# A hybrid conv layer on one Trainium2 core: thirteen rows of norm factors reach all partitions by a store and a repeating load, where a TensorE matmul had spread them

## The chip, the cores and the metric

The kernel runs on one core of one Trainium2 chip. Five engines matter, and each works through its own instruction list in order: TensorE (PE in the profile, with weight loads shown apart as PEld), VectorE (DVE), ScalarE (ACT), GpSimd (POOL) and SyncE (SP), whose instructions here are nearly all DMA issues. The metric is the device time of one execution in microseconds (us). The kernel before takes 1971.13 us, the median of 3 runs that lie between 1970.71 and 1971.24.

## The reference

One layer with a short gated convolution as its token mixer, then a dense SwiGLU feed-forward block, on a sequence of 2048 tokens with 1024 channels in float32. Each of the two sublayers has an RMS norm ahead of it and another behind it, and a shift, a scale and a gate that come from a conditioning vector:

```python
h = modulate(rms_norm(x, norm_gains[i, 0]), sh_m, sc_m)
h = short_conv_mixer(h, conv_w_in[j], conv_w[j], conv_w_out[j])
x = x + g_m[:, None, :] * rms_norm(h, norm_gains[i, 1])
h = modulate(rms_norm(x, norm_gains[i, 2]), sh_f, sc_f)
h = swiglu(h, ffn_w_gate_up[i], ffn_w_down[i])
x = x + g_f[:, None, :] * rms_norm(h, norm_gains[i, 3])
```

An RMS norm needs one number for each token, 1/sqrt(mean of the squares of its 1024 channels). What this case is about is how that number gets from where it is computed to where it is multiplied in.

## The kernel before

**Tiles and stages.** Activations are held channel-major: 128 channels on the partitions, 512 tokens in the free dimension. The 2048 tokens are two units `u` of two groups of 512 (`tok`). The stages run in the order `in0`, `out0`, `in1`, `out1` (the mixer's two projections for unit 0, then unit 1), `gu0`, `down0`, `gu1`, `down1` (the feed-forward block). Each product is a fast block scheme with seven products instead of eight (P1 to P7), and each float32 operand is split in a high and a low part, so that one block product of 128x128 by 128x512 takes three matmuls of reduced precision (`fp32r`).

**Order.** The order on every engine is written out by the program. It runs over a list of slots; one slot is one product, at most 12 matmuls. `later` and `yield n` put a step n slots further on, and the steps that fall due are written out ahead of or behind a slot's matmuls. Weights are fetched some slots ahead of their use (`WHOLE, BLOCKS, SUMS, HIGH, LOW = 5, 9, 7, 5, 4`: whole pairs of high and low part 5 slots ahead, raw blocks 9, the cast to the high part by ACT 5, the low part by DVE 4). Loads and most stores are issued by SP, in that one order, some stores by ACT. The issuing engine waits ahead of an issue for the data, for the buffer and for an earlier DMA: the DMAs of SP and ACT share eight completion counters in turn, and an issue waits until the DMA that had its counter before has landed.

**Norm factors.** The sums of squares of 512 tokens come out with the tokens on the partitions, as a tile of 128x4. `root` turns them into the factors `q`, 128x4 (POOL's power, then three short DVE instructions). The multiplication, though, needs all 512 factors in every partition, as a tile `rb` of 128x512, in a pool with two buffers (`NRB`). `spread_later` does that: DVE writes four diagonal matrices of 128x128 side by side (`diagonal`, names ending in `d`), `lag` slots later TensorE multiplies a matrix of ones with them into a PSUM bank (`spread`, names ending in `b`), and ACT copies the bank to `rb` (names ending in `r`). It is used thirteen times:

- `r2`, `r3` (from `norm_of_rows`): norm ahead of the mixer, unit 1, while `in0` and `out0` run; `lag` is 6.
- `n00`, `n01`, `n10`, `n11` (from `after_out`): norm behind the mixer, in the stages `in1` and `gu0`; `lag` is 4.
- `h00`, `h01`, `h10`, `h11`: norm ahead of the feed-forward block, at the ends of `out1` and `down0`, from factors named `m`; `lag` is 4.
- `o00`, `o01`, `o10` (from `after_down`): norm behind the feed-forward block; `lag` is 4, for `o10` it is 2.

Three more rows of factors are spread elsewhere by TensorE (`r0`, `r1` at the start, `last` at the end). All instructions carry line 78, that of a helper, so names have to tell them apart.

Of the kernel before, what the change touches and what calls it, by code (L numbers as in the profile page):

```python
# [10 lines left out]
F32 = mybir.dt.float32  # L11
# [4 lines left out]
P = 128  # L16
# [7 lines left out]
CH = 512  # L24
# [11 lines left out]
NBIG, NWP, NRAW, NTMP, NRB = 17, 7, 16, 10, 2  # L36
# [13 lines left out]
def hybrid_conv_layer(  # L50
# [31 lines left out]
    V, A, PE, G, SP = map(Engine, (nc.vector, nc.scalar, nc.tensor, nc.gpsimd, nc.sync))  # L82
# [4 lines left out]
    bigs, pairs, raws, sb = (ctx.enter_context(tc.tile_pool(name=n, bufs=1)) for n in ("bigs", "pairs", "raws", "sb"))  # L87
# [12 lines left out]
    def tmp(name):  # L100
        return sb.tile([P, CH + 2], F32, tag="tmp", bufs=NTMP, name=name)
# [4 lines left out]
    def bank(name):  # L106
        return ps.tile([P, CH], F32, tag="mm", bufs=8, name=name)
# [128 lines left out]
    def diagonal(q, name):  # L236
        dg = tmp(name + "d")
        for t in range(4):
            V.tensor_scalar(dg[:, t * P : (t + 1) * P], ident, q[:, t : t + 1], None, ALU.mult)
        return dg  # L240

    def spread(dg, name):
        ps_ = bank(name + "b")
        PE.matmul(ps_, one, dg[:, :CH], start=True, stop=True)
        rb = sb.tile([P, CH], F32, tag="rb", bufs=NRB, name=name + "r")
        A.copy(rb, ps_)
        return rb

    def spread_later(q, name, put, lag=4):
        dg = diagonal(q, name)  # L250
        yield lag
        put(spread(dg, name))

    def norm_of_sums(acc, name):

# [8 lines left out]
    def norm_of_rows(g, name, put):  # L264
        s = [small(4, f"{name}a{i}") for i in range(2)]
        rows = [(t, i) for t in range(4) for i in range(2)]
        xr = {}

        def load(k):
            if k < len(rows):  # L270
                t, i = rows[k]
                xr[k] = raw(f"xr{g}{t}{i}")
                r0 = g * CH + t * P
                SP.dma_start(xr[k], x[r0 : r0 + P, i * CH : (i + 1) * CH])

        load(0)
        yield 2
        for k, (t, i) in enumerate(rows):
            load(k + 1)
            yield 2  # L280
            A.activation(xr[k], xr[k], AF.Square, scale=1.0 / 32.0, accum_out=s[i][:, t : t + 1])
        yield 1
        v = small(4, name + "v")
        V.tensor_tensor(v, s[0], s[1], ALU.add)
        V.tensor_scalar(v, v, EPS, None, ALU.add)
        yield 1
        q = yield from root(v, name)
        yield 1
        yield from spread_later(q, name, put, 6)


    def scratch(shape, name):
        return dram.tile(shape, F32, name=name)
# [598 lines left out]
    for s in slots:  # L892
        ph = s.ph
        if ph.kind in ("out", "down"):
            w = Weight(ph.kind, s.grp, s.op, None, ks=s.ks)
        elif s.n < LEAD and ph.name != "in0" or ph.name == "in1" and s.g.i == 2:
            w = Weight(ph.kind, s.grp, s.op, None)
        else:
            b = of.setdefault((ph.name, s.n), Blocks(ph.kind, s.grp))
            w = Weight(ph.kind, s.grp, s.op, b, ph.name == "in0" and s.g.i in (1, 2),  # L900
                       whole_words=ph.name == "in0" and s.n < LEAD and s.op in UNSPLIT)
# [3 lines left out]
        if s.n >= LEAD and extra.get(ph.name) and len(position) > 7 * LEAD + 2 * (EARLY - LEAD):  # L905
            n = count[ph.name] = count.get(ph.name, 0) + 1
# [26 lines left out]
    def put(d, key, rb):  # L933
        d[key] = rb

    def after_out(ph, tok):
# [4 lines left out]
        q = yield from norm_of_sums(ph.acc[tok], f"n{u}{tok}")  # L941
        yield (24 if u == 0 else 34) + 8 * tok
        yield from spread_later(q, f"n{u}{tok}", partial(put, rb, 0))
        acc = {}
        tiles = {}
# [23 lines left out]
    def after_down(ph, tok):  # L969
# [8 lines left out]
        if not ph.last:  # L978
            yield 22 + 10 * tok
        yield from spread_later(q, f"o{u}{tok}", partial(put, rb, 0), 2 if ph.last else 4)  # L980
        tiles = {}

# [370 lines left out]
    for ph in phases[1:]:  # L1353
# [18 lines left out]
        else:  # L1372
            rb = {}
# [105 lines left out]
```

## Time and profile before

| | before |
|---|---|
| time, median of 3 runs | 1971.13 us |
| the profiled execution, first to last instruction | 1972.0 us |
| PE busy | 1940.5 us (98%), 8460 matmuls |
| DVE busy | 1466.1 us (74%), 2159 instructions |
| ACT busy | 871.4 us (44%), 1430 instructions |
| POOL busy | 340.7 us (17%) |
| DMA | 459.51 MB, mean 233 GB/s |
| granted TensorE clock, mean | 0.997 |

The span of the profiled execution runs from its first to its last instruction; the profile gives no time around it, and it lies 0.9 us above the median of the runs. Busy shares are means over stages with different limits. The views that say more are the busy time by stretches, the chain that ended last (what each step waited for, followed back from the end) and the order of single instructions in a few places.

### The profile page before, as it was taken

The numbers are of one execution on the slowest core, as the hardware profiler recorded it, in microseconds if no ns is written. First come the engines' busy times: TensorE is split into PE (matmuls) and PEld (weight loads), VectorE is DVE, ScalarE is ACT, GpSimd is POOL, SyncE is SP. The second block draws the span as 40 slices with busy tenths as digits, with TensorE's granted clock in tenths as the row PEclk, the third lists the DMA queues.
The fourth block names the chain that finished last, engine by engine and source line by source line (L and its number), as shares of the span: only waits on it lengthen the run. The fifth ranks groups of instructions, "written<-read, shape, count | busy, mean of one in ns | idle before, by whom it ended". The sixth has DMA issues, their size and how long they took to land.

```text
span 1972.0 us, 24969 instructions
## 1 busy us (share of the span) xinstructions
PE 1940.5 (98%) x8460; PEld 1573.3 (80%) x8460; DVE 1466.1 (74%) x2159; ACT 871.4 (44%) x1430; POOL 340.7 (17%) x224
## 2 busy tenths in 40 slices
PE   7899999999999999999999999999999999999998
PEld 4578887777888888888888888888888888888886
DVE  4898888988998876898776755586776655665466
ACT  4543447534345653444333454463333333444452
POOL 0012202201221311243341310120100100111010
PEclk9999999999999999999999999999999999999999
DMA  9369859869996763677665887578564342386634
GB/s 389 126 224 374 312 187 350 320 226 367 327 320 221 272 245 126 231 238 244 210 221 190 295 291 269 188 272 277 187 197 141 122 145 97 115 313 228 199 134 132
DMA packets 204752, 459.51 MB, mean 233 GB/s; under 512 B 22864, under 2 KB 38352, under 8 KB 198224
## 3 DMA queue, kind: packets, MB, share of 16 engines
q1 hardware_dynamic: 180000, 403.52, 59.3%
q10 hardware_dynamic: 24624, 54.40, 7.2%
q8 instruction: 66, 1.08, 0.2%
q14 instruction: 62, 0.51, 0.1%
HBM read 326.75 MB, written 131.07 MB: 232 GB/s over the span
## 4 chain that ended last, share of the span: by engine, by line
PE 84%; DVE 6%; DMA 5%; issue 2%; ACT 2%; SPq 0%; POOL 0%; ACTq 0%; POOLq 0%; DVEq 0%
PE gu0P L78 21%; PE gu1P L78 21%; PE in0P L78 11%; PE down0P L78 11%; PE down1P L78 9%; PE in1P L78 5%; PE out1P L78 4%; PE out0P L78 1%; DMA kgu2P<-gu2P 1%; DVE ada L78 1%; DVE in1c L78 1%; DVE in1y L78 0%; DMA y1S<-in1b1s 0%; DMA in0a<-xt_d 0%; DMA c<-c_row_d 0%
## 5 line engine op out<-in xcount | busy, mean ns | idle before, releaser
L78 DVE TENSOR_TENSOR gu1a<-gu1P,gu1a 128x512 f32<-128x512 f32 x63 | 43.5, 691 | 108.6 <-PE gu1P L78 108.6
L78 DVE TENSOR_TENSOR gu0a<-gu0P,gu0a 128x512 f32<-128x512 f32 x63 | 43.3, 688 | 70.5 <-PE gu0P L78 68.5
L78 POOL TENSOR_TENSOR gu1a<-gu1a 128x512 f32<-128x512 f32 x11 | 19.0, 1728 | 363.4 <-DVE gu1g11s L78 42.5
L78 ACT COPY gu1a<-gu1P 128x512 f32<-128x512 f32 x42 | 24.7, 589 | 98.5 <-PE gu1P L78 87.3
L78 POOL TENSOR_TENSOR nq<-nq,nq 128x512 f32<-128x512 f32 x28 | 42.5, 1517 | 129.9 <-ACT nq L78 125.1
L78 ACT COPY gu0a<-gu0P 128x512 f32<-128x512 f32 x42 | 24.5, 588 | 83.7 <-PE gu0P L78 82.5
L78 DVE CUSTOM_DVE_ANT_0 ada<-ada,c 128x512 f32<-128x512 f32 x80 | 56.8, 720 | 0.0
L78 ACT COPY gu1g<-gu1P 128x512 f32<-128x512 f32 x24 | 14.1, 589 | 92.8 <-PE gu1P L78 92.8
L78 POOL TENSOR_TENSOR down0q<-down0q,down0q 128x512 f32<-128x512 f32 x14 | 23.9, 1705 | 144.1 <-ACT down0q L78 144.0
L78 ACT COPY gu0g<-gu0P 128x512 f32<-128x512 f32 x24 | 14.1, 589 | 76.9 <-PE gu0P L78 75.4
L78 POOL TENSOR_TENSOR gu0a<-gu0a 128x512 f32<-128x512 f32 x11 | 18.3, 1660 | 171.1 <-ACT gu0a L78 47.4
L78 POOL TENSOR_TENSOR down1q<-down1q,down1q 128x512 f32<-128x512 f32 x10 | 16.1, 1610 | 148.7 <-ACT down1q L78 148.6
L78 DVE TENSOR_TENSOR gu1g<-gu1P,gu1g 128x512 f32<-128x512 f32 x24 | 16.6, 692 | 27.4 <-ACT gu1g L78 26.0
L78 DVE TENSOR_TENSOR down2P<-down2P,down2P 128x512 fp32r<-128x512 f32 x14 | 11.9, 853 | 28.6 <-ACT down2P L78 28.6
L78 ACT ACTIVATE gu1a<-gu1a 128x512 f32<-128x512 f32 x42 | 26.6, 633 | 13.2 <-DVE xo L78 6.0
L78 ACT ACTIVATE gu0a<-gu0a 128x512 f32<-128x512 f32 x42 | 26.6, 634 | 11.1 <-DVE gu0a L78 9.3
L78 POOL TENSOR_TENSOR out1q<-out1q,out1q 128x512 f32<-128x512 f32 x14 | 22.3, 1592 | 52.0 <-ACT out1q L78 51.9
L78 POOL TENSOR_TENSOR out0q<-out0q,out0q 128x512 f32<-128x512 f32 x14 | 23.1, 1647 | 44.1 <-ACT out0q L78 44.0
L78 DVE TENSOR_TENSOR xx<-xx,zz 128x512 f32<-128x512 f32 x32 | 28.1, 878 | 1.1
L78 ACT ACTIVATE nq<-xx 128x512 f32<-128x512 f32 x32 | 20.2, 632 | 17.1 <-DVE xx L78 17.0
L78 DVE TENSOR_TENSOR gu0g<-gu0P,gu0g 128x512 f32<-128x512 f32 x24 | 16.5, 689 | 14.7 <-ACT gu0g L78 13.3
L78 DVE TENSOR_TENSOR down10P<-down10P,down10P 128x384 fp32r<-128x384 f32 x14 | 8.6, 615 | 22.3 <-ACT down10P L78 22.3
(3225 smaller groups left out, 6733.5 us busy)
## 6 DMA issues: line engine op xcount, KB each, us to landing
ada<-ada_d SPq DMA_DIRECT2D x64, 256.0 KB, 5.7
act0A<-gu0a SPq DMA_DIRECT2D x33, 256.0 KB, 3.4
act1A<-gu1a SPq DMA_DIRECT2D x33, 256.0 KB, 2.5
ada<-ada_d SPq DMA_DIRECT2D x16, 512.0 KB, 9.4
zz<-z SPq DMA_DIRECT2D x32, 256.0 KB, 5.3
xx<-xt_d SPq DMA_DIRECT2D x32, 256.0 KB, 5.4
x<-xx ACTq DMA_DIRECT2D x32, 256.0 KB, 5.5
down0S<-act0S SPq DMA_DIRECT2D x8, 1024.0 KB, 7.0
```

What stands on the lines that cost most here:

```text
L78: return tc.keep_in_program_order(f(*args, **kwargs))
```

## The change

`spread_later` no longer builds diagonals. It takes a row of 512 floats in device memory, issues from SP a store of the 128x4 factors into it (so that token t·128+p lands at that position: 512 pieces of 4 bytes), and `lag - 1` slots later a load, again from SP, that repeats the row in all 128 partitions of `rb` (128 rows of 2 KB, 256 KB). One slot after that `rb` is handed on, at the same slot as before.

```diff
     def spread_later(q, name, put, lag=4):
-        dg = diagonal(q, name)
-        yield lag
-        put(spread(dg, name))
+
+        row = scratch([CH], name + "w")
+        SP.dma_start(row.rearrange("(t p) -> p t", p=P), q)
+        yield lag - 1
+        rb = sb.tile([P, CH], F32, tag="rb", bufs=NRB, name=name + "r")
+        SP.dma_start(rb, row.rearrange("(a n) -> a n", a=1).to_broadcast((P, CH)))
+        yield 1
+        put(rb)
```

In all, 13 matmuls of 128x512 (each on the profile as two), 52 diagonal blocks on DVE and 13 copies on ACT go; 26 DMAs on SP come. Nothing else changes its order on any engine.

TensorE, near the end of the stage `down1`, around the spread of `o10` (numbers behind names are buffers). Before:

```order
L78 MATMUL down1P_2_15693<-down1S31h,down6P_15671 128x512 x2
L78 MATMUL down1P_2_15693<-down1S_15575,down6P_15671 128x512
L78 MATMUL o10b<-o10d,one 128x512
L78 MATMUL down1P_3_15719<-down1S31h,down7P_15689 128x512 x2
L78 MATMUL down1P_3_15719<-down1S_15575,down7P_15689 128x512
```

After:

```order
L78 MATMUL down1P_2_15633<-down1S31h,down6P_15611 128x512 x2
L78 MATMUL down1P_2_15633<-down1S_15515,down6P_15611 128x512
L78 MATMUL down1P_3_15659<-down1S31h,down7P_15629 128x512 x2
L78 MATMUL down1P_3_15659<-down1S_15515,down7P_15629 128x512
L78 MATMUL down1P_3_15659<-down1S31h,down7P_15629 128x512 x2
```

The spread stood between the products of two groups, and they now follow one another.

SP, at the same place. `down1A` are feature loads, `down1P` to `down9P` weight blocks, `xo` the residual for the output. Before:

```order
L78 DMA down1A_15737<-act1A_123 128x2048
L78 DMA down8P_15754<-kdown8P_9341 128x384
L78 DMA down1A_15759<-act1A_123 128x2048
L78 DMA down1P_15782<-kdown1P_7935 128x512
L78 DMA down1A_15789<-act1A_123 128x1536
L78 DMA down5P_15803<-kdown5P_8741 128x512
L78 DMA xo_15815<-x_134 128x512
L78 DMA down9P_15829<-kdown9P_9554 128x384
```

After:

```order
L78 DMA down1A_15677<-act1A_123 128x2048
L78 DMA down8P_15694<-kdown8P_9301 128x384
L78 DMA down1A_15699<-act1A_123 128x2048
L78 DMA o10w<-o10q 128x4x1
L78 DMA down1P_15719<-kdown1P_7895 128x512
L78 DMA down1A_15726<-act1A_123 128x1536
L78 DMA o10r<-o10w 128x512
L78 DMA down5P_15742<-kdown5P_8701 128x512
L78 DMA xo_15750<-x_134 128x512
L78 DMA down9P_15764<-kdown9P_9514 128x384
```

The store `o10w` waits for the factors `o10q` and stands ahead of a weight block and the third feature load; the load `o10r` waits for the store to land, two issues later, and stands ahead of all that follows.

SP again, in the stage `in1`, around `n01`. `in7P…k` are pairs of weights, `in2b` raw weight blocks, `zz` and `xx` inputs of the residual sum. Before:

```order
L78 DMA xx_4163<-xt_d 128x512
L78 DMA in7P5k<-kin7P_1537 128x1024
L78 DMA in2b_4212<-w_in_d 128x512
L78 DMA in2b_4214<-w_in_d 128x512
L78 DMA in2b_4216<-w_in_d 128x512
L78 DMA zz_4221<-z_128 128x512
L78 DMA xx_4222<-xt_d 128x512
L78 DMA in7P3k<-kin7P_1610 128x1024
```

After:

```order
L78 DMA xx_4148<-xt_d 128x512
L78 DMA n01w<-n01q 128x4x1
L78 DMA in7P5k<-kin7P_1537 128x1024
L78 DMA in2b_4194<-w_in_d 128x512
L78 DMA in2b_4196<-w_in_d 128x512
L78 DMA in2b_4198<-w_in_d 128x512
L78 DMA zz_4203<-z_128 128x512
L78 DMA xx_4204<-xt_d 128x512
L78 DMA n01r<-n01w 128x512
L78 DMA in7P3k<-kin7P_1610 128x1024
```

Here six issues lie between store and load, and the pair `in7P5k` now stands behind the store, `in7P3k` behind the load.

## Prediction, made before the changed kernel was run

> **What bounds the kernel now.** I read the page first, for the busy shares and the chain that ended last.
>
> ```profile
> PE 1940.5 (98%) x8460; PEld 1573.3 (80%) x8460; DVE 1466.1 (74%) x2159; ACT 871.4 (44%) x1430; POOL 340.7 (17%) x224
> PE 84%; DVE 6%; DMA 5%; issue 2%; ACT 2%; SPq 0%; POOL 0%; ACTq 0%; POOLq 0%; DVEq 0%
> ```
>
> TensorE is busy nearly throughout, and 84% of the chain is matmuls. A mean hides the stages, so next came the busy time by stretches (columns: stretch in us, its length, then busy us and instructions of PE, PEld, DVE, ACT and POOL, granted clock, DMA share, GB/s).
>
> ```profile
> 270.00:340.00 70.00, 68.15 (x296) 55.12 (x296) 59.17 (x102) 46.79 (x87) 12.45 (x8) 1.00 0.76 274
> 340.00:420.00 80.00, 77.24 (x344) 62.54 (x343) 72.46 (x111) 42.30 (x66) 18.79 (x11) 1.00 0.86 306
> 420.00:470.00 50.00, 47.56 (x207) 38.39 (x206) 43.45 (x81) 18.29 (x32) 2.92 (x2) 1.00 0.77 263
> 470.00:520.00 50.00, 50.00 (x220) 40.88 (x219) 48.77 (x72) 20.89 (x36) 11.24 (x8) 1.00 0.94 341
> 520.00:570.00 50.00, 49.78 (x227) 41.15 (x227) 49.45 (x74) 18.69 (x34) 14.81 (x10) 1.00 0.99 342
> 570.00:680.00 110.00, 110.00 (x486) 90.25 (x485) 97.80 (x161) 64.15 (x109) 22.20 (x14) 1.00 0.73 253
> 1900.00:1955.00 55.00, 55.00 (x245) 44.71 (x244) 36.53 (x53) 22.95 (x34) 5.09 (x4) 1.00 0.36 114
> ```
>
> There are two regimes. From 570 to 1955 us PE never stands idle (the two rows shown are the first and the last of that stretch; those between read the same), and nine of the thirteen spreads lie there: h00, h01, n10, n11, h10, h11, o00, o01, o10. From 270 to 570 us PE is idle for 1.85 + 2.76 + 2.44 + 0 + 0.22 = 7.3 us, DVE is busy up to 99%, the DMA engines up to 99%: here the limit changes hands, and r3, n00 and n01 lie here. r2 lies just ahead of it, at 268 us.
>
> The chain in order of time (start, us, what) shows which spreads are on it.
>
> ```profile
> 268.43 0.86 PE r2b L78 x2
> ...
> 442.97 0.79 DVE n00d L78 x4
> ...
> 444.39 8.44 DMA y1S<-in1b1s
> ...
> 459.99 7.58 DMA in6P3k<-kin6P
> ...
> 653.87 0.86 PE h00b L78 x2
> 654.72 16.34 PE out1P L78 x72
> ...
> 1910.47 0.86 PE o10b L78 x2
> ```
>
> Twelve of the thirteen spreads stand in it as a piece of PE of 0.86 us (r2b, h00b and o10b shown). The thirteenth, n00, is there too, but by its diagonals on DVE, and behind them the chain runs through landings of DMAs.
>
> **The change part by part.** *The matmul that goes.* Its records overlap, so I take the step between starts on PE (start, us, engine, operation):
>
> ```profile
> 268.03 0.40 PE L78 MATMUL in0P<-in0S2l,in11P 128*128 128x512 f32 x1
> 268.26 1.02 PE L78 MATMUL r2b<-r2d,one 128*128 128x512 f32 x2
> ...
> 269.60 0.40 PE L78 MATMUL in0P<-in0S3l,in11P 128*128 128x512 f32 x1
> ```
>
> From the third matmul of one block to the third of the next are 269.60 − 268.03 = 1.57 us. Three plain steps are 3 × 16.34 / 72 = 0.68 us, so the spread holds PE up for 0.89 us; the chain says 0.86. I take 0.88. Nine times that is 7.9 us in the stretch in which PE never waits. r2, r3 and n01 are on the chain as PE work too: 3 × 0.88 = 2.6 us. For n00 what counts is the 0.79 us of its diagonals. Sum of what goes: 7.9 + 2.6 + 0.8 = 11.3 us. The other diagonals (13 times four blocks of about 0.28 us) and 13 copies on ACT I cost at nothing, since PE covers them; in the 300 us where DVE is the limit they may give something: bounds 0 and 2 us.
>
> *What comes: the load.* The trace has loads of the same shape from one row, and stores to device memory of which only the size differs (last column: us from issue to landing).
>
> ```profile
> c<-c_row_d SPq DMA_DIRECT2D x8, 256.0 KB, 5.4
> z<-down0z SPq DMA_DIRECT2D x16, 256.0 KB, 2.8
> in0c<-xt_d SPq DMA_DIRECT2D x1, 1024.0 KB, 10.7
> q1 hardware_dynamic: 180000, 403.52, 59.3%
> ```
>
> The load lands in about 5.4 us. *The store* has 512 pieces of 4 bytes, which no row shows. Bounds: 2.8 us, as 128 long rows; 10.7 us, the slowest megabyte, which the packet size of 403.52 MB / 180000 = 2.2 KB makes about 470 packets. I take 5 us, nearer to the short store, since so few bytes move.
>
> *Does anyone wait for the pair?* Store and load lie three slots apart for `lag` 4, and a slot is 12 × 16.34 / 72 = 2.72 us: 8.2 us, enough for a store of 5 us. Above 8.2 us SP stands at the load, and behind it all loads of weights. A pair of weights is issued five slots, 13.6 us, ahead of its use and took 7.58 us to land in the chain's row, so SP may stand for some 6 us more before PE is late. For the upper bound, 10.7 us, SP stands 2.5 us: still covered.
>
> *Does the store wait for its factors?* For n, h, o00 and o01 they are long there; n00 is typical, with 65 us between factors and diagonals. For r2 and o10 they are made where the store stands, and SP runs ahead of DVE:
>
> ```profile
> L78 DVE SCALAR_TENSOR_TENSOR n00q<-n00t,n00p x1: 164/164/164, 377.7 to 377.7; 128x4 f32<-128x4 f32 x1
> L78 DVE SCALAR_TENSOR_TENSOR r2q<-r2t,r2p x1: 165/165/165, 250.3 to 250.3; 128x4 f32<-128x4 f32 x1
> 246.41 0.63 SPq L78 DMA_DIRECT2D out1P<-w_out_d  x1
> ...
> 252.83 0.33 SPq L78 DMA_DIRECT2D out1P<-w_out_d  x1
> 260.06 0.33 SPq L78 DMA_DIRECT2D out0A<-y0A  x1
> ```
>
> r2w would stand where SP issued out1P at 246.41, and has to wait until 250.5: 4 us. SP then issued nothing from 253.2 to 260.06, in which it catches up, so I cost that at nothing; without this cover it would be 4 us. The larger wait is at o10:
>
> ```profile
> 1873.01 0.38 SPq L78 DMA_DIRECT2D down1A<-act1A  x1
> 1875.32 0.32 SPq L78 DMA_DIRECT2D down1P<-kdown1P  x1
> 1882.11 0.32 SPq L78 DMA_DIRECT2D down1A<-act1A  x1
> 1901.39 0.16 DVE L78 SCALAR_TENSOR_TENSOR o10q<-o10t,o10p 128x4 f32<-128x4 f32 x1
> 1912.37 1.49 ACT L78 CAST down1A222h<-down1A 128x1536 fp32r<-128x1536 f32 x1
> 1920.08 0.75 DVE L78 SCALAR_TENSOR_TENSOR down1z<-down1z,mG,o10r 128x512 f32<-128x512 f32 x1
> 1927.50 0.62 PE L78 MATMUL down1P<-down1A222h,down8P 128*128 128x512 f32 x2
> ```
>
> SP issued past this point at 1873.4 and will now stand there until 1901.6, 28 us. Queued behind: the weight block down1P, the third feature load, then o10r, more weights and the residual. The feature load, at 1882.11 before, goes out at about 1902.5; if it takes as long as the pair of weights above, 7.6 us, it lands at 1910, 2 us ahead of ACT's cast, and behind that PE has until 1927.50. o10r goes out when the store has landed, 1901.6 + 5 = 1907, and lands at 1912, 8 us ahead of its first use. So the 28 us are covered too, and I cost them at nothing; cover gone, the feature load would have to be some 10 us later before PE stands.
>
> *What the pairs cost the DMA engines.* At 0.4 to 0.7 of their time taken they have room. From 470 to 570 us they have not, and from 420 the chain runs through landings. A load of 256 KB at 342 GB/s is 0.8 us of all 16 engines. A store is 32 pieces per engine; an average packet took 0.593 × 1972.0 × 16 / 180000 = 0.104 us, so at most 3.3 us, at least about nothing. Two pairs (n00, n01): 1.6 to 8.2 us. How much of it reaches PE is open: only one wait of PE for a DMA in this stretch is on record,
>
> ```profile
> PE in1P L78 <- DMA in6P3k<-kin6P: 1.2, 1, 1.2
> ```
>
> which says that the slack is about zero at one point, not everywhere. I take the low end, 1.6 us, since pieces of 4 bytes carry a five-hundredth of the average packet.
>
> *Sum.* 1972.0 − 11.3 + 1.6 = 1962.3 us for an execution like the profiled one, which lay 0.9 us above the median of 1971.13: 1961.4 us.
>
> **The rivals.** *B, the crowded stretch takes most of it back.* The two pairs in in1 cost their upper bound, because landings in turn release SP there: 1971.1 − 11.3 + 8.2 = 1968.0. For it: DMA share of 0.94 to 0.99, and a chain whose steps are landings of 6 to 8 us. Against it: PE waits for a DMA once in 300 us, for 1.2 us.
>
> *C, slower: slow stores hold SP until PE runs out of weights.* If a piece of 4 bytes costs far more than an average packet, the landing L of the store decides: each of twelve loads with three slots or more holds SP for L − 8.2, PE is late from L = 14.2 on, and the gain is gone at 12 × (L − 14.2) = 11.3, L = 15.1 us. At L = 18, 1971.1 − 11.3 + 46 = 2006. Against it: no group of DMAs in the trace, whatever its size, has a median over 10.7 us. No row shows pieces this small, so it keeps a small chance. The Trainium skill speaks for this side: "DMA: Bandwidth & Descriptors", Rules for kernel authors, says that a last dimension that is not contiguous becomes one descriptor per element and should be rearranged, and its Specifications say that below 512 B a write is done as read-modify-write. No trace here shows it yet.
>
> *D, no change: PE's time is not the limit that the 98% suggest*, and something else (DVE's evacuations, weights) sets the pace, so PE only waits 0.88 us more at each place: 1971. Against it: in 570 to 1955 us no wait of PE at all, and twelve of thirteen spreads on the chain as PE. The Trainium skill warns here ("Perfetto Trace Analysis", Identifying the Most-Contended Engine) that matmul busy time is a poor measure, since matmuls are pipelined. That is why I went by steps between starts and by waits, not by the 98%.
>
> **How the numbers follow.** The forecast (most of 11.3 us kept) gets 0.68, B 0.17, C 0.09, D 0.06. The forecast's own range: low, all thirteen at 0.88 (11.4) plus 2 us from DVE, 1957.7; high, half of B's cost, 1971.1 − 11.3 + 4.1 = 1963.9. To hold eight in ten it must reach through B: 1957.5 to 1969.0. What a measurement can tell is about 0.2%, 3.9 us: faster means below 1967.2. The forecast and about half of B lie below: 0.76 faster. The rest of B and D: 0.15 within 0.2%. C: 0.09 slower.
>
> **What would show it.** Right: PE busy lower by some 11 us with no new wait from 570 to 1955; stores landing in 2 to 8 us; o10w issued about 28 us behind the issue before it and no PE wait near the end. B: new PE waits for pairs of weights between 440 and 570 us, of 5 us or more. C: store landings over 14 us and PE waiting for weights behind many loads. D: PE's idle time in 570 to 1955 us going from 0 to 8. A stay of SP at r3r, n11r or o10r that reaches PE would refute the slack of 6 us.

## The result

The changed kernel takes 1988.61 us (median of 4 runs, 1986.66 to 1989.30) against 1971.12 us of the kernel before on the same chip: 1.0083 times as long, 95% interval 1.0071 to 1.0094, 17.5 us slower. The forecast was 1961.4 us, in a range from 1957.5 to 1969.0.

The page of the changed kernel, busy times and shares of the chain by engine:

```profile
PE 1935.4 (97%) x8434; PEld 1570.8 (79%) x8434; DVE 1457.3 (73%) x2107; ACT 862.8 (43%) x1417; POOL 342.4 (17%) x224
PE 77%; DVE 9%; DMA 8%; issue 3%; ACT 2%; POOL 0%; SPq 0%; POOLq 0%; ACTq 0%; DVEq 0%
```

The profiled execution spans 1986.8 us (before 1972.0), 14.8 us more, where the times differ by 17.5. In every run that lists both, the span is 1.7 to 2.3 us shorter than the time; so the profiled execution of the kernel before, at 1972.0, was some 2.7 us longer than its median. PE's busy time fell by 5.1 us, its idle time rose from 31.5 to 51.4 us, by 19.9. The 13 matmuls are 13 × 0.88 = 11.4 us, so some 6 us of PE's saving are missing too. The busy time by stretches (columns as in the prediction: stretch, length, PE, PEld, DVE, ACT, POOL, granted clock, DMA share, GB/s) says where:

```profile
270.00:340.00 70.00, 59.16 (x250) 47.66 (x249) 51.54 (x89) 38.14 (x74) 9.42 (x6) 0.93 0.86 256
340.00:420.00 80.00, 77.08 (x343) 62.46 (x343) 70.68 (x104) 45.99 (x71) 20.86 (x13) 1.00 0.87 316
420.00:470.00 50.00, 44.56 (x184) 35.94 (x183) 39.09 (x73) 14.19 (x24) 2.91 (x2) 0.93 0.77 213
470.00:520.00 50.00, 45.35 (x193) 36.82 (x192) 38.04 (x57) 18.22 (x33) 7.63 (x5) 0.97 1.01 312
570.00:680.00 110.00, 109.54 (x484) 89.64 (x484) 96.76 (x162) 56.83 (x97) 18.87 (x13) 1.00 0.83 269
680.00:860.00 180.00, 178.54 (x790) 146.30 (x789) 142.25 (x187) 82.15 (x138) 36.61 (x22) 1.00 0.69 213
860.00:1955.00 1095.00, 1095.00 (x4853) 907.30 (x4852) 739.83 (x968) 460.36 (x731) 194.16 (x124) 1.00 0.63 211
```

PE's idle time rose by 9.0 us in 270 to 340 (where r3 is stored), by 3.0 in 420 to 470 (n00), by 4.7 in 470 to 520 (n01), and by about 3 us in all the rest. The clock is below 1.00 in the same three stretches: PE works slower behind its stops, and that is most of the missing busy time. From 860 us on PE still never waits. PE's waits (engine, tile, releaser: us in total, times, longest):

```profile
PE out0P L78 <- ACT out0z L78: 10.4, 1, 10.4
PE in1P L78 <- ACT in1c L78: 7.5, 4, 4.2
PE in1P L78 <- DMA in7P5k<-kin7P: 3.4, 1, 3.4
```

Before, the first of these was 1.6 us and the second 2.1. The longest is at r3. Four rows of SP's timeline there (start, us, what), then three of ACT's:

```profile
309.88 0.37 SPq L78 DMA_DIRECT2D r3w<-r3q  x1
...
311.87 0.38 SPq L78 DMA_DIRECT2D out0S<-y0S  x1
...
316.65 4.79 SPq L78 DMA_DIRECT2D out2P<-w_out_d  x1
...
328.48 0.41 SPq L78 DMA_DIRECT2D r3r<-r3w  x1
```

```profile
314.73 0.62 ACT L78 CAST out3P<-out3P 128x512 fp32r<-128x512 f32 x1
327.58 1.90 ACT L78 CAST out0S40h<-out0S 128x2048 fp32r<-128x2048 f32 x1 [12.22 <-DMA out0S<-y0S]
329.38 0.58 ACT L78 COPY out0z<-out0P 128x512 f32<-128x512 f32 x1
```

The same cast in the kernel before:

```profile
320.80 1.90 ACT L78 CAST out0S40h<-out0S 128x2048 fp32r<-128x2048 f32 x1 [1.33 <-DMA out0S<-y0S]
```

A feature load of 1 MB (out0S) goes out 2 us behind the store r3w and lands 15.7 us later, at 327.6; the longest of that kind took 7.7 us before. ACT, which works in order, stands 12.2 us at the cast of it (before 1.3). The copy that empties a PSUM bank for PE (out0z) is queued behind the cast, so PE stops. SP is not what PE waits for: it had issued the load 15.7 us earlier. The same place by stretches of 2 us:

```profile
308.00:310.00 2.00, 2.00 (x10) 1.66 (x9) 1.93 (x5) 0.00 (x0) 1.44 (x1) 1.00 0.82 315
310.00:312.00 2.00, 2.00 (x11) 1.65 (x10) 1.99 (x4) 1.46 (x3) 0.74 (x1) 1.00 1.93 156
312.00:314.00 2.00, 2.00 (x11) 1.50 (x10) 1.73 (x2) 2.00 (x5) 1.92 (x2) 1.00 1.21 60
314.00:316.00 2.00, 2.00 (x10) 1.66 (x10) 2.00 (x5) 1.36 (x3) 0.27 (x1) 1.00 0.73 8
...
318.00:320.00 2.00, 1.63 (x8) 1.01 (x6) 0.00 (x0) 0.00 (x0) 0.00 (x0) 1.00 0.45 6
320.00:322.00 2.00, 0.00 (x0) 0.00 (x0) 0.00 (x0) 0.00 (x0) 0.00 (x0) 1.00 0.55 100
322.00:324.00 2.00, 0.00 (x0) 0.00 (x0) 0.00 (x0) 0.00 (x0) 0.00 (x0) 0.87 1.00 324
...
328.00:330.00 2.00, 0.00 (x0) 0.00 (x0) 0.49 (x1) 2.00 (x3) 0.00 (x0) 0.50 1.09 411
330.00:332.00 2.00, 1.98 (x5) 1.60 (x6) 2.00 (x2) 2.00 (x5) 0.00 (x0) 0.50 1.00 413
332.00:334.00 2.00, 2.00 (x7) 1.56 (x6) 2.00 (x5) 1.50 (x3) 0.00 (x0) 0.57 0.98 313
```

The last column shows the first thing: from 315 GB/s the traffic falls to 6 to 8 and is back at 324 only some 12 us behind the store's issue, although several loads are waiting. The column with 1.00 to 0.50 shows the second, the clock: PE stands still from about 320 to 330, and the granted clock is 0.50 until about 333.7, when PE has worked again for 3.7 us. In 330 to 334 PE is busy for 3.98 us, but gets 12 matmuls done, where 20 to 22 are usual. The Trainium skill has this rule ("TensorE: Matmul & The Clock Gate", Part 1: The HAM clock gate): after an idle window of about 3.4 us the clock is halved, and it comes back after as long a stretch of work. The rows agree: 0.87 as the mean of 322 to 324 puts the drop at 323.5, 3.9 us behind the last matmul, and the clock is back after 3.7 us of work.

At n00 (stored at 445.9) the traffic is down to 41 GB/s from 450 to 456. There too ACT stands at a cast, 7.3 us for a DMA, and a copy that PE needs (in1c) is queued behind it, so that PE stops for 4.2 us. The store of n00 lands after 11.8 us, n01's after 14.6, h00's after 15.2. At o00 the same gap of 10 us (38 GB/s from 1354 to 1364) costs nothing: PE is busy in all of it.

### The profile page after: what moved, and what is told of

Same layout as the page of the kernel before. It is cut to its first block, busy times and chain, and to the rows that moved or that the text cites. A ratio compares the mean times of both kernels' runs of the same rounds, so it can differ in the third digit from the quotient of the medians.

```text
span 1986.8 us, 24877 instructions
## 1 busy us (share of the span) xinstructions
PE 1935.4 (97%) x8434; PEld 1570.8 (79%) x8434; DVE 1457.3 (73%) x2107; ACT 862.8 (43%) x1417; POOL 342.4 (17%) x224
## 3 DMA queue, kind: packets, MB, share of 16 engines
q1 hardware_dynamic: 188736, 406.96, 61.8%
## 4 chain that ended last, share of the span: by engine, by line
PE 77%; DVE 9%; DMA 8%; issue 3%; ACT 2%; POOL 0%; SPq 0%; POOLq 0%; ACTq 0%; DVEq 0%
PE gu1P L78 21%; PE gu0P L78 19%; PE down0P L78 11%; PE in0P L78 10%; PE down1P L78 7%; PE in1P L78 4%; PE out1P L78 3%; DVE in1y L78 1%; PE out0P L78 1%; DMA y1S<-in1b1s 1%; DMA ada<-ada_d 1%; DMA out2P<-w_out_d 1%; DVE in1c L78 1%; DMA in2b<-w_in_d 1%; DVE ada L78 1%
## 5 line engine op out<-in xcount | busy, mean ns | idle before, releaser
L78 DVE TENSOR_TENSOR gu1g<-gu1P,gu1g 128x512 f32<-128x512 f32 x24 | 16.6, 692 | 23.2 <-ACT gu1g L78 22.2
L78 DVE TENSOR_TENSOR down2P<-down2P,down2P 128x512 fp32r<-128x512 f32 x14 | 11.9, 853 | 28.6 <-ACT down2P L78 28.6
L78 ACT ACTIVATE gu0a<-gu0a 128x512 f32<-128x512 f32 x42 | 26.5, 632 | 13.1 <-DVE gu0a L78 10.2
```

The lines of the kernel that those rows point to most:

```text
L78: return tc.keep_in_program_order(f(*args, **kwargs))
```

## The experiments

**Theory 1:** while a store of four-byte pieces lands, hardly any other transfer moves, whichever queue it is in; where a stage has no slack, PE stops. **Theory 2:** what costs is the place of 26 more DMAs in SP's order (waits, shared completion counters), not their pieces. The first runs tell these apart, the later ones find which property of the store does it.

**The store by itself.** Behind the last output of the kernel before, stores of 128x4 and of other shapes one after another, each behind a load into the same tile, so that the next issue shows the landing.

```diff
+    def pieces(n, name):
+        fresh()
+        d = scratch([n * P], name)
+        SP.dma_start(d.rearrange("(t p) -> p t", p=P), t0[:, :n])
+    def runs(p, n, name):
+        fresh()
+        SP.dma_start(scratch([p, n], name), t0[:p, :n])
...
+    for i, E in enumerate((SP, A)):
+        pieces(4, f"pL{i}")
+        E.dma_start(scratch([P, CH], f"pM{i}"), t0)
```

> The kernel before, with a row of stores and loads behind its last output, each alone: 512, 128, 256 and 1024 pieces of 4 bytes; 128 pieces of 16, 64, 512 and 2048 bytes; 4 rows of 512 and one row of 2048 bytes; then a store of 512 four-byte pieces with a 256 KB store issued at the same time, once from SP as well, once from ACT; last a load of 512 four-byte pieces. Theory 1 (the small pieces themselves are slow and hold up what is behind them): 512 pieces take about 10 us to land even alone, 128 pieces about 4, 1024 about 19; 128 pieces of 512 bytes under 3 us; the 256 KB store behind the small one lands about 8 us later than alone. Theory 2 (the store is cheap; what hurts is the waits in SP's order and 26 more DMAs in the eight shared counters): 512 pieces alone land in under 4 us, and the 256 KB store behind them within 1 us of its time alone.

SP's timeline, of which the difference of two starts is the landing (pD: 512 pieces of four bytes; pA: 128 pieces; pF: 128 pieces of 16 bytes):

```profile
1972.00 0.38 SPq L78 DMA_DIRECT2D pD<-p  x1
1982.95 0.34 SPq L78 DMA_DIRECT2D p<-c_row_d  x1
...
1997.93 0.32 SPq L78 DMA_DIRECT2D pA<-p  x1
2005.13 0.33 SPq L78 DMA_DIRECT2D p<-c_row_d  x1
...
2032.80 0.32 SPq L78 DMA_DIRECT2D pF<-p  x1
2034.20 0.33 SPq L78 DMA_DIRECT2D p<-c_row_d  x1
```

The store of the change takes 10.9 us (8.6 the second time) on idle DMA engines, 128 such pieces 7.2, 256 pieces 7.9, 1024 pieces 8.8: from 128 up the number hardly matters. The same 512 floats as 128 pieces of 16 bytes take 1.4 us, as four rows of 512 B 1.2. A store of 256 KB issued behind a four-byte one needed 11.6 us from SP and 7.8 us from ACT's queue; alone 2.0. Reading 512 pieces of four bytes took 2.3 us. The DMA engines look idle in most of the 10.9 us: the DMA share (the last column but one) is 0.13 behind the issue at 1972.00, then 0.00 until the store has landed at 1982.95. The two first stretches:

```profile
1972.00:1974.00 2.00, 0.00 (x0) 0.00 (x0) 0.00 (x0) 0.00 (x0) 0.00 (x0) 0.50 0.13 1
1974.00:1976.00 2.00, 0.00 (x0) 0.00 (x0) 0.00 (x0) 0.00 (x0) 0.00 (x0) 0.50 0.00 0
```

**A few against many rows.** The four rows up to 500 us through memory, the other nine by TensorE, and the reverse; the prediction's crowded part against its solid one.

```diff
 def spread_later(q, name, put, lag=4):
+    if name not in ("r2", "r3", "n00", "n01"):    # the second run: "if name in"
+        dg = diagonal(q, name)
+        yield lag
+        put(spread(dg, name))
+        return
     row = scratch([CH], name + "w")
```

> Only r2, r3, n00 and n01 go through device memory, the other nine stay on TensorE. Theory 1 and 2 alike put the loss in the crowded stretch: PE's new idle time of 270 to 570 us (17.8 us) and the clock lost behind it (about 6 us) stay, 4 x 0.88 us are gained: 1971 + 17.8 + 6.3 - 3.5 = 1991.7. A rival that the loss is spread over all thirteen would give 1971 + 4/13 of 17.5, about 1976.

> Only h00, h01, n10, n11, h10, h11, o00, o01 and o10 go through device memory. Theory 1 and 2: the 9 x 0.88 = 7.9 us that the prediction counted are real, less the 1.9 us of new idle time of PE from 570 to 860 us: 1965. If PE's time in the solid stretch were not what sets the end, 1971.

The first four: 1994.22 us, ratio 1.0114 (1.0097 to 1.0130), with the same waits of PE as the whole change (10.4 and 7.5 us). The last nine: 1973.28 us, ratio 1.0006 (0.9997 to 1.0016), where I had expected 1965. The two longest new waits are both in `out1`, 17 to 18 us behind the issues of the stores of h00 and h01:

```profile
PE out1P L78 <- DVE out1z L78: 2.3, 1, 2.3
PE out1P L78 <- ACT out1z L78: 2.2, 1, 2.2
```

PE's idle time in 570 to 860 us is 5.5 us (before 0), and from 860 on 0. So the solid stretch was not as solid as "PE never waits" reads: a lack of waits shows no waiting, not how much slack is behind it. The two parts don't add up either: 22.2 and 1.3 us against 17.5 for all thirteen. What the stores of one part change for those of the other, no run takes apart.

**One row alone.** Only r3 through memory.

```diff
+    if name != "r3":
+        dg = diagonal(q, name)
+        yield lag
+        put(spread(dg, name))
+        return
```

> The kernel before, with r3 alone through memory as the changed kernel does it (512 pieces of 4 bytes), the other twelve by TensorE. Theory 1: one store costs the whole of the wait at out0z, 9 to 10 us of PE, and 3 us more at the lower clock behind it, less 0.9 us: 1981 to 1985. If the loss in the changed kernel needs several stores after one another (r2, r3, n00, n01): under 1975.

1980.92 us, ratio 1.0048 (1.0032 to 1.0063): one store of 2 KB costs 9.5 us. The only long new wait of PE (1.6 us before) is

```profile
PE out0P L78 <- ACT out0z L78: 9.9, 1, 9.9
```

**The store without its use.** The kernel before, and beside each spread by TensorE the store that nobody reads.

```diff
 def spread_later(q, name, put, lag=4):
+    row = scratch([CH], name + "w")
+    SP.dma_start(row.rearrange("(t p) -> p t", p=P), q)
     dg = diagonal(q, name)
     yield lag
     put(spread(dg, name))
```

> The kernel before, all thirteen spreads on TensorE, and beside each the store of 512 four-byte pieces, which nothing reads. Theory 1 (the store holds up all other transfers for about 8 us, wherever they come from): the changed kernel lost 17.5 us beside 11.4 us of PE saved, 29 in all; most of it returns here: 1990 to 2001. Theory 2 (SP standing at the loads until the store has landed): no load stands behind it, so at most SP's waits for r2q and o10q are left: 1971 to 1974.

1997.24 us, ratio 1.0124 (1.0110 to 1.0138): 25.6 us for 13 stores, with no load of them. An issue further on can still wait for such a store, by the shared completion counter. But the loss is there without any load, so neither the load nor SP's stay at it is needed for it. With the 11.4 us that TensorE gains taken off, 1986 is left, within 3 us of the changed kernel.

**The store from another queue.** The changed kernel, with the store issued by ACT.

```diff
-    SP.dma_start(row.rearrange("(t p) -> p t", p=P), q)
+    A.dma_start(row.rearrange("(t p) -> p t", p=P), q)
```

> As the changed kernel, but the store is issued by ACT, in ACT's order and on ACT's queue; the load stays on SP. If the hold-up is in SP's queue alone, SP's loads pass it by: PE's idle time as before, 1971 - 11.4 + 2 = 1962. If it holds up every queue (in e0_probe a 256 KB store from ACT beside the small store took 7.8 us, 2.0 alone): 1982 to 1990. SP's own wait for r2q and o10q goes in both.

1996.83 us, ratio 1.0128 (1.0109 to 1.0146), and PE's wait at out0z is 11.0 us; behind r3's store the traffic falls to 16 GB/s from 316 to 320 us. SP's loads are held up by a store in ACT's queue as by one of its own. Why it takes some 8 us more than the changed kernel, and more than expected, this run doesn't show. The Trainium skill has a statement that fits ("DMA: Bandwidth & Descriptors", Issuing engines are not separate DMA queues): DMAs of all issuing engines run on the same 16 DMA engines, and a second issuer saves issue time only.

**The same row without four-byte pieces.** TensorE turns q into four rows of 128 (a transpose of 128x4), ACT copies them from PSUM, and the store is four rows of 512 B; load and order as in the changed kernel.

```diff
-    row = scratch([CH], name + "w")
-    SP.dma_start(row.rearrange("(t p) -> p t", p=P), q)
+    row = scratch([4, P], name + "w")
+    ps_ = bank(name + "b")
+    PE.transpose(ps_[0:4, :P], q, ident)
+    qr = sb.tile([4, P], F32, tag="qr", bufs=1, name=name + "c")
+    A.copy(qr, ps_[0:4, :P])
+    SP.dma_start(row, qr)
...
```

> All thirteen, but the factors are turned by one small PE transpose into 4 rows of 128, copied by ACT, and stored as 4 pieces of 512 bytes; the load and its place, and so the number of DMAs and SP's waits for factors, stay. Theory 1: no standstill of the DMA engines behind the store, PE idle as in the kernel before, 13 x (0.88 - 0.25) = 8 us less PE: 1963 to 1966. Theory 2: PE's new idle time stays: 1988 + 13 x 0.25 = 1992.

1972.53 us, ratio 0.9999 (0.9990 to 1.0009), short of the 1963 to 1966. The waits behind the store are gone; instead PE, in order as well, stands at the transpose for factors that are not ready:

```profile
PE r3b L78 <- DVE r3q L78: 8.1, 1, 8.1
```

With the transposes of r2 and r3 six slots later (for `lag` 6 the run waits six slots first and then goes on with `lag` 4, so these two rows also arrive four slots later):

> As e3_rows, but for r2 and r3 the small transpose stands six slots later, where TensorE's spread stood before, so that PE does not wait for their factors; the load follows three slots on. Theory 1 (the store in 4-byte pieces was the loss, PE's time is real): the 8.1 us that PE waited for r3q in e3_rows and the clock lost behind it go, and 13 x (0.88 - 0.25) = 8 us are gained: 1962 to 1964. If PE's saved time were lost anyway, 1971.

1966.17 us, ratio 0.997 (0.996 to 0.998): faster than the kernel before by 5.5 us, though 2 us above the 1962 to 1964 expected. With other pieces 26 DMAs on SP, two pairs of them later, do little harm, and the run ahead of this one, with all in the places of the change, has none of the waits behind the store either: Theory 2 falls.

**Which property of the pieces.** Again stores behind the last output: 128 or 512 pieces, of different sizes and distances in memory.

```diff
+    d = scratch([n * P, step], name).rearrange("(t p) a -> p t a", p=P)
+    SP.dma_start(d[:, :, 0:1], t0[:, :n].rearrange("p (t a) -> p t a", a=1))
```

> The kernel before, with stores behind its last output, each alone: 128 pieces of 4, 8 and 16 bytes side by side; 32 and 16 pieces of 4 bytes side by side; 128 pieces of 4 bytes 8, 64 and 512 bytes apart; 512 pieces of 4 bytes 64 and 512 bytes apart; 512 side by side; 128 of 16 bytes. If neighbours are the matter (many pieces that fall into one short stretch of memory follow one another), pieces 64 or 512 bytes apart land in under 2 us, and 16 side by side in about 2. If a piece of 4 bytes is slow in itself, distance changes nothing: 7 to 9 us. 8 bytes side by side lies between 1.4 and 7.2 us in either case.

128 pieces of 4 bytes side by side: 7.5 us; of 8 bytes 2.9, of 16 bytes 1.8. Four-byte pieces 8 bytes apart 3.3 us, 64 bytes apart 1.4. Sixteen of them side by side 1.3, 32 3.3. And the 512 pieces of the change, by their distance:

```profile
2018.71 0.37 SPq L78 DMA_DIRECT2D pI<-p  x1
2020.72 0.34 SPq L78 DMA_DIRECT2D p<-c_row_d  x1
...
2028.64 0.37 SPq L78 DMA_DIRECT2D pK<-p  x1
2037.47 0.33 SPq L78 DMA_DIRECT2D p<-c_row_d  x1
```

64 bytes apart (pI) 2.0 us, side by side (pK) 8.8. So neither the size of a piece nor the number of pieces alone makes it slow: 512 four-byte pieces are quick when they lie apart, and 128 of 16 bytes when side by side. What is slow is many small pieces side by side, from 32 of them on. What in the memory or on the way to it does this, no run shows; nor whether it matters which DMA engine writes which neighbour.

**All thirteen, stored as they lie.** 128 pieces of 16 bytes (each partition's four factors together); the load repeats that row, and VectorE reads it through a view with a step of 16 bytes.

```diff
-    row = scratch([CH], name + "w")
-    SP.dma_start(row.rearrange("(t p) -> p t", p=P), q)
+    row = scratch([P, 4], name + "w")
+    SP.dma_start(row, q)
...
-    put(rb)
+    put(rb[:, :].rearrange("x (p t) -> x t p", t=4))
```

> All thirteen rows go through memory, and TensorE does nothing for them, as in the changed kernel; but the store writes the 128x4 factors as they lie, 128 pieces of 16 bytes, and the multiplication on VectorE reads the repeated row through a view with a step of 16 bytes, so that the right factors are multiplied. Theory 1 (neighbouring pieces of 4 bytes hold up all transfers): stores land in 1.4 to 2.5 us, no wait of PE for out0z or in1c of more than 2 us, PE busy about 1930 us, 1961 to 1964 us, if VectorE reads with a step as fast as before. If the detour through memory is slow as such, or if small stores of any form hold up the rest: 1975 to 1990. If the stepped read of VectorE is slow (twice 0.75 us at 104 places): waits of PE for VectorE in in1 and out1, 1970 and more.

1985.14 us, ratio 1.0070 (1.0058 to 1.0083). At r3 there is no gap that matters (again 2 us each; the lowest of the eleven stretches up to 330 us is the first one shown):

```profile
310.00:312.00 2.00, 2.00 (x11) 1.65 (x10) 1.93 (x6) 0.96 (x2) 0.19 (x1) 1.00 0.45 159
312.00:314.00 2.00, 2.00 (x10) 1.67 (x9) 1.72 (x3) 1.94 (x5) 1.92 (x2) 1.00 0.97 216
314.00:316.00 2.00, 2.00 (x10) 1.51 (x9) 2.00 (x4) 1.91 (x4) 0.81 (x1) 1.00 0.99 265
```

and PE's wait at out0z is 1.3 us. What is slower is VectorE; the same group in the kernel before, and then in this one (count | busy us, mean ns):

```profile
L78 DVE SCALAR_TENSOR_TENSOR zz<-zz,mG,n00r 128x512 f32<-128x512 f32 x8 | 6.0, 745 | 0.0
```

```profile
L78 DVE SCALAR_TENSOR_TENSOR zz<-zz,mG,n00r 128x512 f32<-128x512 f32 x8 | 9.1, 1136 | 0.0
```

DVE's busy time is 1497.1 us, 40 more than in the changed kernel, and PE waits for it and for ACT in `in1` and `gu0` (longest 3.6 us, for `n00t`); from 470 to 570 us DVE is busy for 98.8 of 100 us.

**The same store, put in order by ACT.** The repeated row goes to a temporary tile, and one ACT copy, as the kernel before had one, brings it into token order; the loads go out one or two slots behind the store.

```diff
+    row = scratch([P, 4], name + "w")
+    SP.dma_start(row, q)
+    early = 1 if lag == 2 or name[0] == "h" else 2
+    yield early
+    raw_ = tmp(name + "k")[:, :CH]
+    SP.dma_start(raw_, row.rearrange("p t -> (p t)").rearrange("(a n) -> a n", a=1).to_broadcast((P, CH)))
+    yield lag - early
+    rb = sb.tile([P, CH], F32, tag="rb", bufs=NRB, name=name + "r")
+    put(rb)
+    copy = lambda: A.copy(rb.rearrange("x (t p) -> x t p", p=P), raw_.rearrange("x (p t) -> x t p", t=4))
+    if name[0] in "no":
+        later(2 if lag == 2 else 1, copy)
+    else:
+        copy()
```

> As the run before (all thirteen rows through memory, stored as 128 pieces of 16 bytes), but the repeated row is put into token order by one ACT copy of 128x512 (as the kernel before had one from PSUM), so that VectorE multiplies from neighbouring elements again; the loads go out one or two slots behind the store instead of three, so that the copy doesn't wait for them. If the 14 us of the run before are the stepped reads of VectorE (1.13 us instead of 0.75): the waits of PE for VectorE and ACT in in1, and those in 680 to 860, go, 1961 to 1965 us. If they come from the detour itself (loads that repeat a row, SP's waits for the store): 1975 or more again. If the loads land late, ACT stands at the copies and PE waits for out0z or out1z: 1967 to 1975.

1962.81 us (1961.09 to 1963.18), ratio 0.9953 (0.9940 to 0.9967) to the kernel before: the fastest of all, 8.1 us below it. Its busy times from the page, then four of the stretches:

```profile
PE 1928.7 (98%) x8434; PEld 1567.6 (80%) x8434; DVE 1455.4 (74%) x2107; ACT 876.0 (45%) x1430; POOL 339.7 (17%) x224
```

```profile
270.00:340.00 70.00, 68.25 (x298) 55.16 (x296) 57.93 (x95) 47.67 (x89) 14.78 (x10) 1.00 0.83 289
340.00:420.00 80.00, 74.99 (x332) 60.52 (x331) 71.25 (x112) 40.58 (x63) 16.46 (x10) 1.00 0.85 302
470.00:520.00 50.00, 50.00 (x227) 41.52 (x226) 47.43 (x68) 20.77 (x35) 11.76 (x9) 1.00 0.99 332
570.00:680.00 110.00, 110.00 (x490) 90.93 (x489) 96.66 (x155) 67.85 (x114) 20.13 (x14) 1.00 0.77 263
```

PE's busy time is down by 11.8 us, its idle time is 32.0 us (before 31.5), and the clock stays at 1.00 in every stretch shown. Of the 11.8 us, 1.6 are the clock's: in the first 100 us the kernel before ran 9.9 us of PE's work at 0.50, this one 6.8, and half of the difference is time. That leaves 10.2 us for the thirteen matmuls, 0.79 each, a little under the prediction's 0.88. This run also has its loads earlier than the run before it, so how the 22 us between them divide over VectorE's reads and that was not measured; VectorE's 42 us less of busy time were.

## Why the prediction was wrong

- **The failed term: what a store costs the DMA engines.** "A store is 32 pieces per engine", at 0.104 us a packet "at most 3.3 us", for two pairs "1.6 to 8.2 us", of which I took 1.6, "since pieces of 4 bytes carry a five-hundredth of the average packet". One store in fact stops nearly all transfers for about 10 us. I priced it by packets and bytes, and added its share to the busy time of the engines; what was needed is how long others stand. Nor did the room that I saw help ("at 0.4 to 0.7 of their time taken they have room"): r3, where the share of the DMA engines was 0.76, lost most.
- **The store's landing.** I took 5 us between bounds of 2.8 and 10.7 ("nearer to the short store, since so few bytes move"). The nine stores whose landing the trace shows took 10.3 to 15.2 us, seven of them above the upper bound; alone it was 8.6 to 10.9 us. Even 10.7 would not have led to the right time, since the landing entered my sum only as a delay of SP.
- **The way to PE.** I looked for lateness in SP and the weights. At the longest wait it came through a feature load and ACT in order: out0S, its cast, behind it the copy out0z. Only 3.4 us came by a pair of weights, which is B's mechanism.
- **The clock was no term at all.** Behind the three stops at r3, n00 and n01 PE did 3.7, 5.8 and 2.8 us of its work at a clock of 0.50 (from 330.0, 461.0 and 515.2 us on). Half of these 12.3 us, 6.2, is lost.
- **What held.** The matmul's price, about: 13 × 0.88 = 11.4, measured 10.2 with the harmless store. PE without a wait from 860 us to the end. The 28 us of SP at o10: o10w went out at 1917.75, 28.6 us behind the issue before it, and no wait of PE followed. The wait of r2w did not reach PE either.
- **The rivals.** C had the right suspicion (four-byte pieces cost far more than an average packet; two of the nine landings were over 14 us) and the wrong path: with the store in ACT's queue, and with no load waiting for it, the loss is the same or larger, so SP's stay is not what costs. The rule of the Trainium skill cited there ("DMA: Bandwidth & Descriptors", Rules for kernel authors: keep the last dimension contiguous) spoke for the right side and points to the form of store that does no harm; but a count of descriptors explains little, since 512 pieces 64 bytes apart take 2.0 us. D doesn't hold: with the harmless store the kernel is 8.1 us faster.

The sum as it came out, for the profiled execution: 1972.0 − 9.7 (matmuls) + 19.9 (more idle time of PE) + 4.6 (PE at a lower clock: 6.2 behind the three stops, less 1.6 in the first 100 us, where the kernel before ran 3.1 us more of its work at 0.50) = 1986.8. The first term is what the others leave. The prediction's last step took 0.9 us off, as if a span could be compared with a time; 2.7 us would have been right, which puts the forecast 1.8 us lower, further from the result.

## What to carry to other kernels

Price an unfamiliar transfer by what stands still while it lands, not by its bytes and packets, and measure it alone first: one run with a few stores behind the kernel's end would have told 10.9 from 1.4 us. Don't scatter single floats over neighbouring places of device memory; store each partition's values as they lie, and reorder them on an engine that has time. An in-order engine carries one late load to every work behind it, so ask of each stage which load its engines stand at first, and how far ahead it is.

## What the runs showed of the hardware

- Stores of four-byte pieces side by side: 128 to 1024 pieces land in 7.2 to 10.9 us, in 1.4 to 2.0 us when 64 bytes or more apart, and in 1.3 us when there are only 16 (32 side by side: 3.3 us).
- Meanwhile transfers from SP's queue and from ACT's stand: 6 to 8 GB/s at the lowest, and 256 KB from ACT's queue in 7.8 us, where the same store from SP took 2.0 alone. The mean packet doesn't show it: the 8736 packets that came with the change (188736 after 180000) raised the time of SP's queue (59.3% of 16 × 1972.0 us to 61.8% of 16 × 1986.8 us) by 0.107 us each, about the 0.104 us of the average packet before. The longest does: 9.8 us in the trace of the changed kernel, 2.2 us before.
- Reading 512 pieces of four bytes took only 2.3 us: the write is what is slow.
- A step of 16 bytes in one of VectorE's float32 inputs raised a 128x512 instruction from 0.745 to 1.136 us; an ACT copy of 128x512 with such a step took 1.13 us, where the plain copy of the kernel before, from PSUM, took 0.58.
